# An SSD layer on one core: the chunk scan woven one filling step later, the gate norm behind a whole z tile, three products moved to VectorE

## The chip, the cores and the metric

The kernel runs on one core of one Trainium2 chip. The metric is the device time of one execution in microseconds, lower is better. The engines of the core are named as in the profile: PE is TensorE (matrix products and transposes), DVE is VectorE, ACT is ScalarE, POOL is GpSimd, and SP is the engine that here only issues DMAs. Each engine works through its own instructions in order; engines wait for one another by semaphores.

## The reference, cut to what matters

One inference step of a streaming encoder: a Mamba-2 SSD layer, an MLP, a stick-breaking attention layer and another MLP, each behind an RMS norm and with a residual. There are 1024 prompt tokens and 32 further tokens with cached state, 1056 in all, and the model width is 1024. Only the SSD layer is touched by the change. Its mixer:

```python
zxbcdt = u @ in_w
z, xbc, dt_raw = jnp.split(zxbcdt, [D_INNER, D_INNER + CONV_DIM], axis=-1)
xbc, new_conv = causal_conv(xbc, conv_state, conv_w, conv_b)
...
h_new = h * jnp.exp(a_cs[:, -1])[..., None, None] + jnp.einsum(
    'bsgn,bsgr,bsgrp->bgrpn', b_c, decay_end, xdt_c)
return h_new, y_diag + y_off
```

The input projection gives z, x, B, C and dt. x, B and C go through a causal convolution of four taps and a silu. Then, for each of 8 groups of 4 heads, a recurrence over the tokens is worked out in chunks: inside a chunk by matrix products of C, B and x with decay factors (`y_diag`), from chunk to chunk by a state h (`y_off`). The result, plus D times x, is multiplied by silu(z), RMS-normalised over each group of 256 channels, scaled by `norm_w` and projected back to the model width by `out_w`.

## The kernel before

Activations lie feature-major: 128 features on the partitions, 1056 tokens along the free dimension. Every large product is an fp32 product made of three matmuls of high and low parts. One tile of 128 output features is worked in three column groups of 352 tokens; eight blocks of 128 input features times three matmuls make 24 matmuls per column group. A tile is given out as six **steps** of 12 matmuls. For the tiles of the input projection (`ps_i`) the evacuation out of PSUM is on VectorE: L451 for z, L411 to L415 for x, B and C. Weights are loaded by L137 (`ws_i`) and split in high and low by ACT (L143) and POOL or DVE (L144).

The SSD layer's main loop (from L613) runs over the 8 groups. In round g it builds two lists and weaves them together:

- `main`, the **filling** of TensorE: the two z tiles of group g-1, and the conv tiles B, C, x0 and x1 of group g+1. Between them stand the three parts of the gate norm. Part a (L552 to L554) multiplies the scan's result by z and forms the squares; it belongs to group g-1. Parts b and c belong to group g-2 by then. Part b (L556 to L562) sums the squares over the channels with eight small matmuls (L227, `ss_g`), takes the reciprocal root in eleven small VectorE operations (L560, L214 to L223) and spreads the rows over the partitions by two DMAs, to DRAM and back (L244 `sd_g`, L247 `gs`). Part c (L564 to L568) multiplies by that (two L566 on VectorE, which wait for the second DMA) and stores the two rows `yn_d`. In round 7 the filling is the z tiles of groups 6 and 7, the gate parts, the loads of the residual X0 and X1 (into the places of `s_6x`, the two x tiles of group 6) and the first six steps of the output projection (`ps_o`, evacuated by L658 into X).
- `side`, the **scan** of group g: 9 chunks (the last one the 32 further tokens), each in a stage A and a stage B, in the order A0, A1, B0, A2, B1, ... A8, B7, B8. Stage A of a chunk loads the decay sums `ab` (L470), multiplies B with C and transposes x0, x1 and B into one PSUM tile `pa` (L475 to L478), forms the decay matrix L (POOL L480 adds the mask, ACT L483 takes exp, DVE L484 multiplies), scales x (two L488, `xd`), copies B (ACT L491, `bt`) and scales C by exp(ab) (ACT L493, POOL L494). Stage B forms the state's increment (L509), the part inside the chunk (L514) and the part from the state (L517, which needs h of the chunk before and the product of L494) in a PSUM tile `pb`; POOL L523 forms `ht`, the decayed old state, DVE L525 adds the increment to give h (L520 for chunk 0), and two L528 add the result to x in place.

`weave(main, side, lead)` calls the main steps one by one and, after each, as many scan stages as keep the two lists in proportion; the first `lead` steps pass without any. So `lead` sets how far stage A of chunk 0 stands behind the start of the round.

Stage A of chunk 0 needs the x1 tile of its own group, whose last filling steps end the round before. After them x1 goes through two taps on VectorE (L427 twice, L430, L431), a tanh on ACT (L432, into `cv`) and the closing product on VectorE (L433, into `s_3x` for group 3).

The order on each engine is that in which a scheduler places the instructions of this program; the queues then work in that order. PSUM tiles `pa` and `pb` have two buffers each, `ps_i` and `ps_o` share four; the gate's `gs` tiles have one each.

Of the kernel before, what the change touches and what calls it, by code (L numbers as in the profile page):

```python
# [12 lines left out]
ALU = mybir.AluOpType  # L13
# [52 lines left out]
def weave(main, side, lead=0):  # L66

    n, m = len(main), len(side)
    j = 0
    for i, f in enumerate(main):  # L70
        f()
        want = max(i + 1 - lead, 0) * m // (n - lead)
        while j < want:
            side[j]()
            j += 1
    while j < m:
        side[j]()
        j += 1
# [16 lines left out]
def hybrid_step(ctx: ExitStack, tc: tile.TileContext, xt, cst, cbf, w_in, w_dt, w_out, w_up0, w_dn0, w_qkv, w_o,  # L95
                w_up1, w_dn1, ssm0, ck, cv, y_o, pssm_o, sssm_o, conv_o, pk_o, v_o):
    nc = tc.nc
    ve, sc, gp, te = nc.vector, nc.scalar, nc.gpsimd, nc.tensor
# [199 lines left out]
    def ssd_layer():  # L298
# [4 lines left out]
        with st:  # L303
# [156 lines left out]
            def scan_thunks(g):  # L460
# [4 lines left out]
                def stage_a(c):  # L465
                    w = 128 if c < 8 else 32
                    tk = slice(128 * c, 128 * c + w)
                    B, C, x0, x1 = (slots[g, k] for k in ("B", "C", "x0", "x1"))
                    ab = qp.tile([128, 4, 128], F32, name=f"ab_{g}_{c}", tag="ab", bufs=3)
# [21 lines left out]
                    sc.activation(bt[0:w, :], A[0:w, 384:512], AF.Copy)  # L491
                    if c > 0:
                        sc.activation(ab[:, :, :w], ab[:, :, :w], AF.Exp)  # L493
                        gp.tensor_tensor(ab[:, :, :w], ab[:, :, :w],  # L494
                                         C[:, None, tk].to_broadcast([128, 4, w]), op=ALU.mult)
                    box[c] = (L, xd, bt, ab)

                def stage_b(c):
                    w = 128 if c < 8 else 32
                    tk = slice(128 * c, 128 * c + w)  # L500
                    L, xd, bt, ce = box.pop(c)
                    if c == 8:
                        h = box["h0"]
                    elif c == 0:
                        h = None
                    else:
                        h = box["h"]
# [11 lines left out]
                    if h is None:  # L519
                        ve.tensor_copy(hn, Bp[:, 256:512])  # L520
                    else:
                        ht = qp.tile([128, 256], F32, name=f"ht_{g}_{c}", tag="ht", bufs=1)
                        gp.tensor_tensor(ht.rearrange("p (h d) -> p h d", d=64), h.rearrange("p (h d) -> p h d", d=64),  # L523
                                         een[:, 4 * g:4 * g + 4, c, None].to_broadcast([128, 4, 64]), op=ALU.mult)
                        ve.tensor_tensor(hn, ht, Bp[:, 256:512], op=ALU.add)  # L525
                    for j in range(2):
# [61 lines left out]
            for i, n in enumerate(("ss", "dt", "tails")):  # L588
# [6 lines left out]
                w = min(512, T - 512 * i)  # L595
# [17 lines left out]
            for g in range(8):  # L613
                main, side = [], scan_thunks(g)
                if g > 0:

                    for j in range(2):
                        z = z_tile(g - 1, j)
                        main += z[:2] + gates[:1] + z[2:]
                        gates = gates[1:]  # L620
                    gates = gate(g - 1)
                if g < 7:
                    for k in ("B", "C", "x0", "x1"):
                        if k == "B" and gates:
                            main.append(gates.pop(0))
                        main += conv_tile(g + 1, k)
                else:
                    gt = gates
                    main += gt[0:1] + z_tile(7, 0) + gt[1:2] + z_tile(7, 1, False) + gt[2:3]
                    out0 = late(lambda: down_block(w_out[0], load_o(yn_d, 0, None, stage(0), 1), X, pg, "o0",  # L630
                                                   gmajor=True), 24)
                    main += [lambda: X.extend(load_x(xt, (2, 3, 4, 5, 0, 1, 6, 7), range(2)))] + out0[:6]
                weave(main, side, 2 if g == 7 else 3)
            eng[0] = ve
            dma(conv_o, cvo)
            gt = gate(7)
# [1118 lines left out]
```

## Time and profile before

| | us |
|---|---|
| runs of the kernel | 3014.51, 3011.33, 3012.99 |
| median | 3012.99 |
| the profiled execution, its own time | 3010.28 |
| the span of its profile | 3008.4 |

The granted TensorE clock was 0.992 in the mean. The part that the change touches, the SSD layer's main loop, runs from about 70 to 790 us of the span. There the profile gives for every group from 2 on the same picture, 91.87 us apart (one and the same step of groups 3 and 4 starts at 336.10 and 427.97), so one group stands for the others.

Read the profile in this order: the page for the share of each engine; the list of what TensorE waited for (its rows read "waiting engine, tile and line <- engine, tile and line that released it"); then the timelines of the engines around such a wait (start, duration, engine, line, operation, "[idle time before <- releaser]"; x8 at the end joins eight instructions); and the chain that ended last for the end of group 7.

### The profile page before, as it was taken

The numbers are of one execution on the slowest core, as the hardware profiler recorded it, in microseconds if no ns is written. First come the engines' busy times: TensorE is split into PE (matmuls) and PEld (weight loads), VectorE is DVE, ScalarE is ACT, GpSimd is POOL, SyncE is SP. The second block draws the span as 40 slices with busy tenths as digits, with TensorE's granted clock in tenths as the row PEclk, the third lists the DMA queues.
The fourth block names the chain that finished last, engine by engine and source line by source line (L and its number), as shares of the span: only waits on it lengthen the run. The fifth ranks groups of instructions, "written<-read, shape, count | busy, mean of one in ns | idle before, by whom it ended". The sixth has DMA issues, their size and how long they took to land.

```text
span 3008.4 us, 54983 instructions
## 1 busy us (share of the span) xinstructions
PE 2939.5 (98%) x22262; PEld 2795.8 (93%) x22262; DVE 2270.4 (75%) x3327; ACT 1288.4 (43%) x2207; POOL 626.3 (21%) x525
## 2 busy tenths in 40 slices
PE   9999999999999999999999999999999999999999
PEld 7898999998999999999998888888889999999999
DVE  7877787777748877788776677667677977788776
ACT  4433343434214333444333466666664433344331
POOL 2766656665100000000000123332230000000000
PEclk9999999999999999999999999999999999999999
DMA  4323333324532543365432322222234434464442
GB/s 139 73 54 86 82 85 67 85 79 121 198 93 86 194 140 136 132 205 167 138 97 101 105 73 73 69 68 72 79 100 162 151 137 157 136 206 153 140 131 75
DMA packets 185589, 349.28 MB, mean 116 GB/s; under 512 B 21132, under 2 KB 78328, under 8 KB 185336
## 3 DMA queue, kind: packets, MB, share of 16 engines
q1 hardware_dynamic: 185336, 345.77, 37.4%
q8 instruction: 175, 2.87, 0.4%
q14 instruction: 78, 0.64, 0.1%
HBM read 240.80 MB, written 96.52 MB: 112 GB/s over the span
## 4 chain that ended last, share of the span: by engine, by line
PE 82%; DVE 11%; issue 2%; DMA 2%; ACT 2%; POOL 0%; SPq 0%; DVEq 0%; ACTq 0%; POOLq 0%
PE ps_i L185 15%; PE ps_ua L887 9%; PE ps_ub L887 9%; PE ps_o L185 3%; PE ps_q L185 3%; PE ps_k L185 2%; PE o L1433 2%; PE wt L1417 2%; PE ps_o L166 2%; PE ps_v L185 2%; PE ps_lb L166 2%; PE ps_la L166 2%; PE ps_p L185 1%; DVE p L1380 1%; PE pb L514 1%
## 5 line engine op out<-in xcount | busy, mean ns | idle before, releaser
L185 PE MATMUL ps_i<-xh_n,wh_i 128*128 128x352 f32 x1056 | 356.2, 337 | 0.0
L185 PE MATMUL ps_i<-xh_n,wl_i 128*128 128x352 f32 x1056 | 340.5, 322 | 0.0
L185 PE MATMUL ps_i<-xl_n,wh_i 128*128 128x352 f32 x1056 | 340.2, 322 | 0.0
L1380 DVE TENSOR_TENSOR_SCAN p<-p 128x255 f32<-128x255 f32 (+7 forms) x128 | 193.3, 1511 | 90.8 <-ACT p L1378 89.8
L1382 POOL TENSOR_TENSOR b<-b,p 128x255 f32<-128x255 f32 (+7 forms) x128 | 165.2, 1291 | 379.9 <-DVE p L1380 231.4
L185 PEld LDWEIGHTS ps_i<-xh_n,wh_i 128*128 128x128 f32 x1056 | 198.9, 188 | 13.3 <-issue 12.0
L185 PEld LDWEIGHTS ps_i<-xl_n,wh_i 128*128 128x128 f32 x1056 | 200.2, 190 | 0.0
L185 PEld LDWEIGHTS ps_i<-xh_n,wl_i 128*128 128x128 f32 x1056 | 198.7, 188 | 0.0
L1254 POOL MEMSET qs<- 128x64 f32 x8 | 1.2, 150 | 872.5 <-PE ss_a L227 855.0
L483 ACT ACTIVATE L<-L,naT 128x128 f32<-128x128 f32 (+1 forms) x288 | 90.2, 382 | 154.2 <-POOL L L480 154.1
L1378 ACT ACTIVATE p<-z,qn_q 128x384 f32<-128x384 f32 (+4 forms) x192 | 104.8, 580 | 60.3 <-PE z L1409 29.4
L144 POOL TENSOR_TENSOR wl_i<-ws_i,wh_i 128x1024 fp32r<-128x1024 f32 x44 | 106.8, 2428 | 73.5 <-ACT wh_i L143 73.2
L480 POOL TENSOR_TENSOR L<-ab,cs 128x512 f32<-128x512 f32 (+1 forms) x72 | 106.2, 1475 | 55.0 <-PE pb L514 41.4
L1417 PE MATMUL wt<-cs,b 128*128 128x128 f32 x576 | 90.4, 280 | 15.4 <-DVE wts L1422 12.9
L1378 ACT ACTIVATE b<-z,qn_q 128x384 f32<-128x384 f32 (+4 forms) x192 | 104.4, 585 | 0.0
L738 ACT ACTIVATE d_a<-y_a 128x528 fp32r<-128x528 f32 x105 | 66.8, 640 | 85.5 <-DMA y_a<-q_da 14.0
L738 ACT ACTIVATE d_b<-y_b 128x528 fp32r<-128x528 f32 x105 | 66.4, 639 | 81.6 <-DMA y_b<-q_db 10.9
L1417 PEld LDWEIGHTS wt<-cs,b 128*128 128x128 f32 x576 | 64.9, 140 | 31.2 <-DVE wts L1422 14.5
L739 DVE TENSOR_TENSOR d_a<-y_a,d_a 128x528 fp32r<-128x528 f32 x105 | 73.4, 704 | 19.2 <-ACT d_a L738 19.1
L739 DVE TENSOR_TENSOR d_b<-y_b,d_b 128x528 fp32r<-128x528 f32 x105 | 73.4, 704 | 18.2 <-ACT d_b L738 18.1
L887 PE MATMUL ps_ua<-b_a,wh_a_raw 128*128 128x264 f32 x480 | 77.2, 282 | 0.0
L887 PE MATMUL ps_ub<-b_b,wh_b_raw 128*128 128x264 f32 x480 | 77.2, 282 | 0.0
(1667 smaller groups left out, 9411.1 us busy)
## 6 DMA issues: line engine op xcount, KB each, us to landing
y_a<-q_da SPq DMA_DIRECT2D x98, 264.0 KB, 3.5
y_b<-q_db SPq DMA_DIRECT2D x98, 264.0 KB, 3.4
ws_i<-in_w_in SPq DMA_DIRECT2D x48, 512.0 KB, 3.7
ab<-acs_d SPq DMA_DIRECT2D x64, 256.0 KB, 5.1
ws_a<-in_w_up SPq DMA_DIRECT2D x30, 512.0 KB, 3.7
ws_b<-in_w_up SPq DMA_DIRECT2D x30, 512.0 KB, 3.7
q_da<-t_a SPq DMA_DIRECT2D x26, 528.0 KB, 3.8
q_db<-t_b SPq DMA_DIRECT2D x26, 528.0 KB, 3.4
```

The costliest lines, as they stand in the source:

```text
L144: eng[0].tensor_tensor(lo, st, hi.bitcast(F32), op=ALU.subtract)
L166: te.matmul(box["ps"][g][:, :GW], a[:, c:c + 128], b[:, GRP[g]], start=(k == ks[0] and i == 0), stop=(k == ks[-1] and i == 2))
L185: te.matmul(box["ps"][:, :n], a[:, c:c + 128], b[:, grp[g]], start=(k == 0 and i == 0), stop=(k == nk - 1 and i == 2))
L480: gp.tensor_tensor(L[0:w, :, :w], ab[0:w, :, :w], cs[0:w, None, C_MASK:C_MASK + w].to_broadcast([w, 4, w]), op=ALU.add)
L483: sc.activation(L[0:w, h, :w], L[0:w, h, :w], AF.Exp, bias=naT[0:w, c, 4 * g + h:4 * g + h + 1])
L738: sc.activation(hi, x, AF.Copy)
L739: ve.tensor_tensor(lo, x, hi.bitcast(F32), op=ALU.subtract)
L887: te.matmul(ps[:, g, :QW], a[:, c:c + 128], b[:, QW * g:QW * g + QW], start=(first and n == 0 and i == 0), stop=(n == len(ks) - 1 and i == 2),
L1378: sc.activation(t[0:np_, c:c + w], ps[0:np_, :w], AF.Sigmoid, scale=sn[0:np_, f])
L1380: ve.tensor_tensor_scan(p[0:np_, 1:W][:, ::-1], p[0:np_, 1:W][:, ::-1], p[0:np_, 1:W][:, ::-1], 1.0, op0=ALU.mult, op1=ALU.bypass)
L1382: gp.tensor_tensor(b[0:np_, 0:W - 1], b[0:np_, 0:W - 1], p[0:np_, 1:W], op=ALU.mult)
L1417: te.transpose(ps[:, c, :], self.b[:, 128 * (c0 + c):128 * (c0 + c) + 128], ident)
```

## The change

Four edits, all inside the SSD layer.

```diff
--- before.py
+++ after.py
@@ -491,8 +491,8 @@
                     sc.activation(bt[0:w, :], A[0:w, 384:512], AF.Copy)
                     if c > 0:
                         sc.activation(ab[:, :, :w], ab[:, :, :w], AF.Exp)
-                        gp.tensor_tensor(ab[:, :, :w], ab[:, :, :w],
-                                         C[:, None, tk].to_broadcast([128, 4, w]), op=ALU.mult)
+                        (ve if (g, c) == (7, 8) else gp).tensor_tensor(
+                            ab[:, :, :w], ab[:, :, :w], C[:, None, tk].to_broadcast([128, 4, w]), op=ALU.mult)
                     box[c] = (L, xd, bt, ab)
 
                 def stage_b(c):
@@ -520,7 +520,7 @@
                         ve.tensor_copy(hn, Bp[:, 256:512])
                     else:
                         ht = qp.tile([128, 256], F32, name=f"ht_{g}_{c}", tag="ht", bufs=1)
-                        gp.tensor_tensor(ht.rearrange("p (h d) -> p h d", d=64), h.rearrange("p (h d) -> p h d", d=64),
+                        (ve if g == 7 and c > 6 else gp).tensor_tensor(ht.rearrange("p (h d) -> p h d", d=64), h.rearrange("p (h d) -> p h d", d=64),
                                          een[:, 4 * g:4 * g + 4, c, None].to_broadcast([128, 4, 64]), op=ALU.mult)
                         ve.tensor_tensor(hn, ht, Bp[:, 256:512], op=ALU.add)
                     for j in range(2):
@@ -616,7 +616,7 @@
 
                     for j in range(2):
                         z = z_tile(g - 1, j)
-                        main += z[:2] + gates[:1] + z[2:]
+                        main += z + gates[:1]
                         gates = gates[1:]
                     gates = gate(g - 1)
                 if g < 7:
@@ -630,7 +630,7 @@
                     out0 = late(lambda: down_block(w_out[0], load_o(yn_d, 0, None, stage(0), 1), X, pg, "o0",
                                                    gmajor=True), 24)
                     main += [lambda: X.extend(load_x(xt, (2, 3, 4, 5, 0, 1, 6, 7), range(2)))] + out0[:6]
-                weave(main, side, 2 if g == 7 else 3)
+                weave(main, side, 4)
             eng[0] = ve
             dma(conv_o, cvo)
             gt = gate(7)
```

In words. (1) The weave's lead is 4 steps in every round, instead of 3 (2 in round 7). (2) In each round with z tiles, gate parts b and c stand behind the six steps of their z tile instead of after the first two. (3) In group 7 the small product of L494 for the last chunk, exp(ab) times C (128 x 4 x 32), is given to VectorE. (4) So are, in group 7, the products `ht` of L523 for chunks 7 and 8 (128 x 256).

How the order moves, first on VectorE at the start of round 3. Here `s_3x_3292` is x1 of group 3, `z_3345` the first z tile of group 2, `gs_1` the gate tile of group 1, `L_0` and `xd_0` stage A of chunk 0. Before:

```order
L431 SCALAR_TENSOR_TENSOR s_3x_3292<-pre_90,cwh,cv_3x_3288 128x32
L560 TENSOR_SCALAR gs_1_2677<-ss_g_3347 128x264
L214 TENSOR_SCALAR gs_1_2677<-gs_1_2677 128x264
L215 TENSOR_SCALAR gs_1_2677<-gs_1_2677 128x264
L216 SCALAR_TENSOR_TENSOR gs_1_2677<-gs_1_2677 128x264
L433 SCALAR_TENSOR_TENSOR s_3x_3292<-cv_3x_3288,s_3x_3292 128x1056
L217 TENSOR_TENSOR gs_1_2677<-gs_1_2677 128x264
L451 SCALAR_TENSOR_TENSOR z_3345<-ps_i_1_3366,rstd 128x352
L218 SCALAR_TENSOR_TENSOR gs_1_2677<-gs_1_2677 128x264
L484 TENSOR_TENSOR L_0_3399<-L_0_3399,pa_0_3394 128x512
```
After, the same place:

```order
L431 SCALAR_TENSOR_TENSOR s_3x_3292<-pre_90,cwh,cv_3x_3288 128x32
L433 SCALAR_TENSOR_TENSOR s_3x_3292<-cv_3x_3288,s_3x_3292 128x1056
L451 SCALAR_TENSOR_TENSOR z_3345<-ps_i_1_3347,rstd 128x352
L451 SCALAR_TENSOR_TENSOR z_3345<-ps_i_2_3373,rstd 128x352
L484 TENSOR_TENSOR L_0_3409<-L_0_3409,pa_0_3404 128x512
L488 TENSOR_TENSOR xd_0_3416<-pa_0_3404,dtT 128x256
L488 TENSOR_TENSOR xd_0_3416<-pa_0_3404,ddT 128x256
L455 SCALAR_TENSOR_TENSOR z_3345<-zt_3399,z_3345 128x1056
L560 TENSOR_SCALAR gs_1_2677<-ss_g_3421 128x264
L484 TENSOR_TENSOR L_1_3466<-L_1_3466,pa_1_3461 128x512
L214 TENSOR_SCALAR gs_1_2677<-gs_1_2677 128x264
```
The product L433 that ends x1 now stands directly behind L431. The gate's chain (L560, L214 and on) begins behind the z tile's product L455 and runs through stage A of chunk 1.

Second, on VectorE some twenty rows on, at the two L566 of group 1's gate. `h_1` is the state after chunk 1, `z_3492` the second z tile. Before:

```order
L566 SCALAR_TENSOR_TENSOR s_1x_1281<-s_1x_1281,cs,gs_1_2678 128x1056
L566 SCALAR_TENSOR_TENSOR s_1x_1469<-s_1x_1469,cs,gs_1_2678 128x1056
L484 TENSOR_TENSOR L_2_3528<-L_2_3528,pa_2_3523 128x512
L488 TENSOR_TENSOR xd_2_3535<-pa_2_3523,dtT 128x256
L488 TENSOR_TENSOR xd_2_3535<-pa_2_3523,ddT 128x256
L451 SCALAR_TENSOR_TENSOR z_3492<-ps_i_1_3508,rstd 128x352
L525 TENSOR_TENSOR h_1_3578<-ht_1_3579,pb_1_3568 128x256
L528 SCALAR_TENSOR_TENSOR s_3x_3141<-s_3x_3141,cs,pb_1_3568 128x128
L528 SCALAR_TENSOR_TENSOR s_3x_3292<-s_3x_3292,cs,pb_1_3568 128x128
L451 SCALAR_TENSOR_TENSOR z_3492<-ps_i_2_3555,rstd 128x352
```
After:

```order
L451 SCALAR_TENSOR_TENSOR z_3492<-ps_i_1_3494,rstd 128x352
L484 TENSOR_TENSOR L_2_3550<-L_2_3550,pa_2_3545 128x512
L488 TENSOR_TENSOR xd_2_3557<-pa_2_3545,dtT 128x256
L488 TENSOR_TENSOR xd_2_3557<-pa_2_3545,ddT 128x256
L451 SCALAR_TENSOR_TENSOR z_3492<-ps_i_2_3530,rstd 128x352
L566 SCALAR_TENSOR_TENSOR s_1x_1260<-s_1x_1260,cs,gs_1_2678 128x1056
L566 SCALAR_TENSOR_TENSOR s_1x_1469<-s_1x_1469,cs,gs_1_2678 128x1056
L455 SCALAR_TENSOR_TENSOR z_3492<-zt_3577,z_3492 128x1056
L525 TENSOR_TENSOR h_1_3594<-ht_1_3595,pb_1_3584 128x256
L528 SCALAR_TENSOR_TENSOR s_3x_3141<-s_3x_3141,cs,pb_1_3584 128x128
L528 SCALAR_TENSOR_TENSOR s_3x_3292<-s_3x_3292,cs,pb_1_3584 128x128
```
The two L566 have moved behind the last evacuation L451 of the second z tile; L455 stands right behind them, and L525 of `h_1`, which stood ahead of that evacuation and of L455, now stands behind all of these.

Third, on VectorE at the end of group 7, where `s_6x` are the tiles of gate 6, `wl_o_2` the low part of a weight of the output projection, `xl_y` the low parts of its input, `h_7` and `h_8` the states after chunks 7 and 8. Before:

```order
L566 SCALAR_TENSOR_TENSOR s_6x_5910<-s_6x_5910,cs,gs_6_7314 128x1056
L566 SCALAR_TENSOR_TENSOR s_6x_6061<-s_6x_6061,cs,gs_6_7314 128x1056
L525 TENSOR_TENSOR h_6_7683<-ht_6_7684,pb_6_7673 128x256
L528 SCALAR_TENSOR_TENSOR s_7x_6833<-s_7x_6833,cs,pb_6_7673 128x128
L528 SCALAR_TENSOR_TENSOR s_7x_6984<-s_7x_6984,cs,pb_6_7673 128x128
L484 TENSOR_TENSOR L_8_7754<-L_8_7754,pa_8_7749 32x4x32
L488 TENSOR_TENSOR xd_8_7761<-pa_8_7749,dtT 32x256
L488 TENSOR_TENSOR xd_8_7761<-pa_8_7749,ddT 32x256
L144 TENSOR_TENSOR wl_o_2_7990<-ws_o_2_7987,wh_o_2_7989 128x1024
L205 TENSOR_TENSOR xl_y_8084<-yl_sp_8081,xh_y_8083 128x1056
L205 TENSOR_TENSOR xl_y_8090<-yl_sp_8087,xh_y_8089 128x1056
L525 TENSOR_TENSOR h_7_7806<-ht_7_7807,pb_7_7796 128x256
```
After:

```order
L144 TENSOR_TENSOR wl_o_2_7990<-ws_o_2_7987,wh_o_2_7989 128x1024
L566 SCALAR_TENSOR_TENSOR s_6x_5910<-s_6x_5910,cs,gs_6_7293 128x1056
L566 SCALAR_TENSOR_TENSOR s_6x_6061<-s_6x_6061,cs,gs_6_7293 128x1056
L525 TENSOR_TENSOR h_6_7727<-ht_6_7728,pb_6_7717 128x256
L528 SCALAR_TENSOR_TENSOR s_7x_6833<-s_7x_6833,cs,pb_6_7717 128x128
L528 SCALAR_TENSOR_TENSOR s_7x_6984<-s_7x_6984,cs,pb_6_7717 128x128
L484 TENSOR_TENSOR L_8_7768<-L_8_7768,pa_8_7763 32x4x32
L488 TENSOR_TENSOR xd_8_7775<-pa_8_7763,dtT 32x256
L488 TENSOR_TENSOR xd_8_7775<-pa_8_7763,ddT 32x256
L494 TENSOR_TENSOR ab_8_7761<-ab_8_7761,s_7C 128x4x32
L523 TENSOR_TENSOR ht_7_7821<-h_6_7727,een 128x256
L205 TENSOR_TENSOR xl_y_8084<-yl_sp_8081,xh_y_8083 128x1056
```
The weight's L144 has moved ahead of the two L566, and L494 and the first L523 stand between them and `h_7`, which follows one L205 later; the second L523 and a third L205 come after that, ahead of `h_8`.

On TensorE the gate's L227 (`ss_g`) stands behind stage A of chunk 0, where it stood behind the first 24 matmuls of the z tile. On SP's queue the weight load L137 that stood between the spread's two DMAs (L244 and L247) in rounds 2 to 6 now stands ahead of both.

## The prediction

> **What bounds the kernel now.** The page comes first, for the share of each engine.
>
> ```profile
> span 3008.4 us, 54983 instructions
> PE 2939.5 (98%) x22262; PEld 2795.8 (93%) x22262; DVE 2270.4 (75%) x3327; ACT 1288.4 (43%) x2207; POOL 626.3 (21%) x525
> ```
>
> TensorE (PE) is busy for 98% of the span, and the change adds and removes no matmul. It can move the time only through the microseconds in which TensorE waits. The second view is the list of what PE waited for in the first 1200 us, which hold the whole SSD stage (columns: us in total, times, longest).
>
> ```profile
> PE pa L477 <- DVE s_2x L433: 2.9, 1, 2.9
> PE pb L517 <- POOL ab L494: 2.2, 1, 2.2
> PE ps_o L185 <- DVE X_in_xt L658: 1.9, 1, 1.9
> PE pa L477 <- DVE s_3x L433: 1.8, 1, 1.8
> PE pa L477 <- DVE s_4x L433: 1.8, 1, 1.8
> PE pa L477 <- DVE s_5x L433: 1.8, 1, 1.8
> PE pa L477 <- DVE s_7x L433: 1.8, 1, 1.8
> PE pa L477 <- DVE s_6x L433: 1.8, 1, 1.8
> PE pa L477 <- DVE s_0x L433: 1.5, 1, 1.5
> PE pa L477 <- DVE s_1x L433: 1.5, 1, 1.5
> ```
>
> In each of the eight groups the transpose of x1 in stage A of chunk 0 (L477) waits until VectorE has finished x1's silu (L433): 2.9 + 5 x 1.8 + 2 x 1.5 = 14.9 us. The rows with L494 and L658 are the end of group 7. The sum thus has three kinds of term: these waits, waits that the new order makes, and the end of group 7.
>
> **Lead and gate part: the waits that go (L633, L619).** The third view is the timeline of group 3, VectorE, ScalarE and TensorE around that wait.
>
> ```profile
> 333.00 1.08 ACT L432 ACTIVATE cv_3x<-s_3x 128x1056 f32<-128x1056 f32 x1 [5.24 <-DVE s_3x L431]
> 334.36 1.25 DVE L433 SCALAR_TENSOR_TENSOR s_3x<-cv_3x,s_3x 128x1056 f32<-128x1056 f32 x1
> 335.67 0.33 PE L477 MATMUL pa<-cs,s_3x 128*128 128x128 f32 x1 [1.84 <-DVE s_3x L433]
> 335.83 0.27 PE L478 MATMUL pa<-cs,s_3B 128*128 128x128 f32 x1
> 339.78 0.38 PE L475 MATMUL pa<-s_3C,s_3B 128*128 128x128 f32 x2
> ```
>
> Without the wait L477 would have run at 335.67 - 1.84 = 333.83. From L478 to the next stage A lie 24 matmuls of the filling, 339.78 - 335.83 = 3.95 us, so one step of 12 is 1.96 us. Now six steps stand ahead of stage A of chunk 0 instead of four, while the column sum L227 (about 0.6 us) goes behind it: it comes to L477 at 333.83 + 3.92 - 0.6 = 337.2. L433 can start when the tanh ends, 334.08, and the four gate instructions that stood ahead of it are gone: it ends at 335.4. That leaves 1.8 us to spare in groups 3 to 6, about 0.4 in group 2 (3.3 more against 2.9), and 1.96 - 1.5 = 0.4 in groups 0 and 1, where one step is added. In group 7 three steps are added. I take all eight waits as gone: **-14.9 us**. If a group's margin is not there, it keeps part of its 1.5 to 2.9.
>
> Group 2 has something behind its wait.
>
> ```profile
> 242.32 0.48 PE L477 MATMUL pa<-cs,s_2x 128*128 128x128 f32 x1 [2.87 <-DVE s_2x L433]
> 242.59 0.42 PE L478 MATMUL pa<-cs,s_2B 128*128 128x128 f32 x1
> 247.90 0.39 PE L475 MATMUL pa<-s_2C,s_2B 128*128 128x128 f32 x2
> 200.00:250.00 50.00, 47.13 (x325) 43.73 (x325) 40.77 (x64) 18.44 (x34) 26.32 (x24) 0.97 0.27 64
> ```
>
> The same 24 matmuls took 247.90 - 242.59 = 5.31 us instead of 3.95, with a granted clock (the column 0.97) below 1 in that stretch: the wait of 2.87 us cost **1.4 us** more, which goes with it. The Trainium skill ("TensorE: Matmul & The Clock Gate", section "What's actually happening") gives half clock after an idle window of about 3.4 us; by it a wait of 2.87 us need cost nothing and the sum would be 1.4 us smaller, but the rows of this trace show the dip after the shorter wait, and the measurement decides; that result, 3003.9, lies within the case that I forecast.
>
> In group 0 the copy of B for chunk 1 (L491) now stands behind the tanh L432 on ScalarE. The 1.08 us of L432 bounds it; most of it lies beside the filling, and I take 0.3.
>
> **The same edits: the wait they can make.** The gate part that moves issues eight small matmuls, eleven VectorE operations (L560, L214 to L223), two DMAs of the spread (L244, L247), and behind it come two L566 and two stores (L568). All of it begins later. On VectorE the two L566, which wait for the spread, and the z product L455 now stand ahead of the state h of chunk 1 (L525), which stage B of chunk 2 needs (L517); before, h came behind L566 too, but with time to spare.
>
> ```profile
> 336.64 0.68 DVE L484 TENSOR_TENSOR L<-L,pa 128x512 f32<-128x512 f32 x1
> 339.38 0.43 DVE L223 SCALAR_TENSOR_TENSOR gs<-gs 128x264 f32<-128x264 f32 x1
> 343.41 0.33 SPq L137 DMA_DIRECT2D ws_i<-in_w_in  x1
> 343.83 0.38 SPq L247 DMA_DIRECT2D gs<-sd_g  x1
> 344.57 2.44 POOL L552 TENSOR_TENSOR s_2x<-s_2x,z 128x1056 f32<-128x1056 f32 x1 [1.19 <-DVE z L455]
> 348.26 2.93 DVE L566 SCALAR_TENSOR_TENSOR s_1x<-s_1x,cs,gs 128x1056 f32<-128x1056 f32 x2 [1.92 <-DMA gs<-sd_g]
> 360.53 0.39 PE L517 MATMUL pb<-ab,h 128*64 128x128 f32 x4
> 796.50 0.43 DVE L223 SCALAR_TENSOR_TENSOR gs<-gs 128x264 f32<-128x264 f32 x1
> 802.25 1.32 DVE L566 SCALAR_TENSOR_TENSOR s_7x<-s_7x,cs,gs 128x1056 f32<-128x1056 f32 x1
> L455 DVE SCALAR_TENSOR_TENSOR z<-zt,z x16: 1243/2600/2892, 155.6 to 760.7; 128x1056 f32<-128x1056 f32 x16
> ```
>
> L517 of that stage comes one step later and without the wait: 360.53 + 1.96 - 1.84 = 360.65. VectorE's side, walked from the last z evacuation at 336.6: that evacuation and stage A of chunk 0 (0.5, then L484's 0.68 and two products like L525's 0.41), L455 at 2.6 (its median; 1.24 when GpSimd is idle) to 341.2, then 2.4 of GpSimd's product L552, beside which the first gate operation may stand still as L494 does below, to 343.7, then thirteen short operations (L223's 0.43 at most, less where they overlap) to some 348.9. The spread took 348.26 - 339.81 = 8.45 us before, because its second DMA stood on SP's queue behind L137, which waited; where nothing stood ahead it took 802.25 - 796.93 = 5.3. In the new order L137 stands ahead of both, where its wait is over by then, so I take 5.3: L566 from 354.2 to 357.1, L455 to 358.4 or 359.7, h at 358.8 or 360.1. The need is at 360.65, so the margin is 0.5 to 1.8 us, within the error of such a walk: bounds 0 and, with a spread of 8.45, 360.1 + 3.15 - 360.65 = 2.6 us in each of six groups. I take 0.4 each, **+2.5 us**.
>
> **Two products on VectorE, and the end of group 7 (L494, L523).** Rows of GpSimd, TensorE, VectorE, and of the chain that ended last.
>
> ```profile
> 761.91 2.54 DVE L566 SCALAR_TENSOR_TENSOR s_6x<-s_6x,cs,gs 128x1056 f32<-128x1056 f32 x2
> 764.37 0.41 DVE L525 TENSOR_TENSOR h<-ht,pb 128x256 f32<-128x256 f32 x1
> 764.47 4.02 DMA yn_d<-s_6x
> 766.25 4.47 POOL L494 TENSOR_TENSOR ab<-ab,s_7C 128x128 f32<-128x128 f32 x1 [1.50 <-ACT ab L493]
> 766.87 1.20 DVE L144 TENSOR_TENSOR wl_o<-ws_o,wh_o 128x1024 fp32r<-128x1024 f32 x1
> 768.00 2.41 DVE L205 TENSOR_TENSOR xl_y<-yl_sp,xh_y 128x1056 fp32r<-128x1056 f32 x2
> 768.56 4.51 DMA X_in_xt<-in_xt
> 770.78 0.31 PE L517 MATMUL pb<-ab,h 128*64 128x32 f32 x4 [2.22 <-POOL ab L494]
> 773.55 15.78 PE ps_o L185 x84
> ```
>
> GpSimd's small L494 took 4.47 us because L144 and L205 ran on VectorE meanwhile; on VectorE it should take about 0.35 (near the L525 row's 0.41 for twice the width), and the two L523 0.41 each: 1.2 us more on VectorE, and the wait of 2.22 goes. But TensorE then waits for the same end as before: L185 needs a PSUM slot, which L658 frees once X0 is loaded into the place of s_6x, and that follows L566, the store of 4.02 and the load of 4.51. So removing 2.22 us gains nothing by itself. And L566 comes later: a product L144 (1.20) now stands ahead of it, and h of chunk 3 with its two L528 (1.0, of which 0.3 found a gap) is now done behind the gate's column sum, on a VectorE without a gap. That is 1.9 us, so L658 goes from 773.1 to 775.0. VectorE itself, with 1.2 + one further L205 (1.2) ahead of L658, is there at 775.3. TensorE resumes near 775.6 instead of 773.55: 2 us. Its 84 matmuls took 15.78 instead of 84 x 1.96 / 12 = 13.7 after two waits of 2.2 and 1.9; a longer one can cost up to 2 more, half of it taken: **+3 us**, bounds 0 (L144 falls into a gap) and 6 (the load collides with the weights' load).
>
> **Sum.** -14.9 - 1.4 + 0.3 + 2.5 + 3 = -10.5 us. Against the profiled execution's own 3010.28 us this is 2999.8. The median of the runs, 3012.99, lies 2.71 above that execution, so for a median I say **3002.5 us**.
>
> **Rivals.**
> - All waits go and none comes: -16.3 + 0 to 1.5 in group 7, 2996.7 to 2998.2. For it: every margin in the walk is positive. Against: the X0 chain is bound to L566.
> - The new wait for h is 1 to 2.5 us in groups 2 to 7, 6 x 1.75 = 10.5 instead of 2.5: -2.5, 3010.5. For it: the margin of 0.5 us in the slow case, and L455's median of 2.6.
> - Slower: the same place, with the spread at 8.45 us or more because SP's queue is held up there too. It decides when L223 to L566 exceeds 5.8 us in the slow case of L455. Then 6 x 2.6 = 15.6, and a wait of that size has the 1.4 us of group 2 behind it: 6 x 1.4 = 8.4. With 0.3 + 5 in group 7 that is -16.3 + 29.3 = +13, 3026. Against: L137 has left the place between the spread's DMAs.
> - The change does not do what it says: stage A of chunk 0 still waits in groups 0 to 2, where 0.4 us is to spare, and the end of group 7 keeps its wait under the name L658. About half of 5.9 + 1.4 comes back, -7, 3006.
>
> **Chances.** Forecast 0.43 (2998 to 3006), all gone 0.18, waits for h 0.20, slower 0.08, partly 0.11. The measurement of this kernel can tell some 0.2%, 6 us, from no change: under 3007 is faster, over 3019 slower. Faster: 0.43 + 0.18 + 0.05 of the partial case = 0.66; slower 0.07; the rest 0.27. The range 2994 to 3012 leaves out the slower case and the edges.
>
> **What would show it.** In the list of waits: no row L477 from L433 (part 1); a row L517 from DVE h L525 in groups 2 to 7 if the spread is late, with L566 directly behind "DMA gs" on VectorE; the row L517 from POOL L494 gone, and L658's grown from 1.9 to 4 or more. The windows at 200 to 250 should show clock 1.00. The forecast is wrong if L223 to L566 takes over 6 us, or if x1's silu still comes last in a group with 0.4 us to spare.

## The result, and the profile after

The changed kernel took 2995.81 us (median of 6 runs, 2993.78 to 3000.29) against 3012.01 (median of 6 runs of before, 3004.58 to 3014.51): a ratio of 0.995, 95% interval 0.9939 to 0.996, 16 us less. In a later comparison the same kernel took 2998.78 against 3011.3, ratio 0.9958 (0.9944 to 0.9972), 13 us less. The forecast was 3002.5, 10.5 less.

First the page of the kernel after.

```profile
span 2991.5 us, 54964 instructions
PE 2932.9 (98%) x22262; PEld 2789.3 (93%) x22262; DVE 2278.7 (76%) x3330; ACT 1286.2 (43%) x2207; POOL 637.1 (21%) x522
```

The matmuls are as many as before, the span is 16.9 us shorter. Next the list of what TensorE waited for in the first 1200 us, after (columns as before: in all, times, longest).

```profile
PE ps_o L185 <- DVE X_in_xt L658: 4.1, 1, 4.1
PE pb L517 <- DVE h L525: 2.1, 6, 0.5
PE pb L509 <- DVE s_7x L528: 1.1, 1, 1.1
PE ps_o L185 <- DVE xl_y L205: 0.9, 1, 0.9
PE pb L509 <- ACT bt L491: 0.5, 1, 0.5
PE pa L477 <- DVE s_0x L433: 0.5, 1, 0.5
```

Seven of the eight rows L477 are gone, and group 0 keeps 0.5. The new row is L517 from h, 2.1 us in six small pieces; L494 is gone, and L658 has grown from 1.9 to 4.1. Before, these rows and their like came to 14.9 + 2.2 + 1.9 = 19.0 us; now they come to 9.2, which is 9.8 less. (A second execution of each kernel, below, gives 19.6 and 10.4, 9.2 less.)

Where does that stand in the span? A good landmark is the first of the matmuls of the first MLP shown here (L887 with `b_a`; the MLP itself begins 8.7 us ahead of it, in both kernels): up to there lies all that the change touches, behind it instructions that the change leaves alone. Before, then after (the numbers ahead of the semicolon are its first and last start):

```profile
L887 PE MATMUL ps_ua<-b_a,wh_a_raw x480: 278/283/285, 986.6 to 1282.4; 128*128 128x264 f32 x160
```

```profile
L887 PE MATMUL ps_ua<-b_a,wh_a_raw x480: 278/283/285, 976.6 to 1272.4; 128*128 128x264 f32 x160
```

The SSD stage thus gave 10.0 us in this pair of executions, and 16.9 - 10.0 = 6.9 us came from later stages whose instructions are the same. So there were two questions for the experiments: which edit brings the 10 us, and where the other 6.9 come from. Two stretches of the same work in the attention stage show the latter's face (last columns: granted TensorE clock, DMA share, GB/s). Before:

```profile
1650.00:1700.00 50.00, 48.33 (x299) 44.49 (x297) 24.01 (x54) 18.01 (x41) 3.46 (x7) 0.93 0.33 91
```

After, the same work, ten us earlier, and the stretch of group 2:

```profile
200.00:250.00 50.00, 50.00 (x356) 46.39 (x354) 41.61 (x61) 18.59 (x38) 31.27 (x25) 1.00 0.31 76
1640.00:1690.00 50.00, 48.33 (x318) 43.85 (x318) 25.95 (x58) 20.75 (x49) 4.32 (x8) 1.00 0.34 97
```

TensorE was as busy in both (48.33 us), but before it had a clock of 0.93: 0.07 x 50 = 3.5 us lost there. In what follows, a stretch in which the granted clock falls below 1 is called a clock dip.

### The profile page after: what moved, and what is told of

It is laid out like the page before. It is cut to its first block, busy times and chain, and to the rows that moved or that the text cites. A ratio compares the mean times of both kernels' runs of the same rounds, so it can differ in the third digit from the quotient of the medians.

```text
span 2991.5 us, 54964 instructions
## 1 busy us (share of the span) xinstructions
PE 2932.9 (98%) x22262; PEld 2789.3 (93%) x22262; DVE 2278.7 (76%) x3330; ACT 1286.2 (43%) x2207; POOL 637.1 (21%) x522
## 3 DMA queue, kind: packets, MB, share of 16 engines
q8 instruction: 175, 2.87, 0.4%
## 4 chain that ended last, share of the span: by engine, by line
PE 66%; DVE 7%; issue 2%; DMA 2%; ACT 2%; POOL 1%; SPq 0%; DVEq 0%; ACTq 0%; POOLq 0%
PE ps_ua L887 9%; PE ps_ub L887 9%; PE ps_q L185 3%; PE ps_o L185 3%; PE ps_i L185 2%; PE ps_k L185 2%; PE o L1433 2%; PE wt L1417 2%; PE ps_o L166 2%; PE ps_lb L166 2%; PE ps_la L166 2%; PE ps_v L185 2%; PE ps_p L185 1%; DVE p L1380 1%; PE ps_k L166 1%
## 5 line engine op out<-in xcount | busy, mean ns | idle before, releaser
L185 PEld LDWEIGHTS ps_i<-xh_n,wh_i 128*128 128x128 f32 x1056 | 198.3, 188 | 13.1 <-issue 12.5
L480 POOL TENSOR_TENSOR L<-ab,cs 128x512 f32<-128x512 f32 (+1 forms) x72 | 115.1, 1599 | 49.7 <-PE pb L514 28.6
L144 POOL TENSOR_TENSOR wl_i<-ws_i,wh_i 128x1024 fp32r<-128x1024 f32 x44 | 106.7, 2426 | 49.6 <-ACT wh_i L143 49.4
L1417 PE MATMUL wt<-cs,b 128*128 128x128 f32 x576 | 90.3, 280 | 14.9 <-DVE wts L1422 12.4
L658 DVE TENSOR_TENSOR X_in_xt<-X_in_xt,ps_o 128x352 f32<-128x352 f32 x72 | 35.6, 518 | 54.9 <-PE ps_o L185 31.6
L887 PE MATMUL ps_ub<-b_b,wh_b_raw 128*128 128x264 f32 x480 | 77.3, 283 | 0.0
```

Source lines behind the costliest of these rows:

```text
L144: eng[0].tensor_tensor(lo, st, hi.bitcast(F32), op=ALU.subtract)
L185: te.matmul(box["ps"][:, :n], a[:, c:c + 128], b[:, grp[g]], start=(k == 0 and i == 0), stop=(k == nk - 1 and i == 2))
L480: gp.tensor_tensor(L[0:w, :, :w], ab[0:w, :, :w], cs[0:w, None, C_MASK:C_MASK + w].to_broadcast([w, 4, w]), op=ALU.add)
L887: te.matmul(ps[:, g, :QW], a[:, c:c + 128], b[:, QW * g:QW * g + QW], start=(first and n == 0 and i == 0), stop=(n == len(ks) - 1 and i == 2),
L1417: te.transpose(ps[:, c, :], self.b[:, 128 * (c0 + c):128 * (c0 + c) + 128], ident)
```

## The experiments

In the table "first L887" is that landmark in the one profiled execution of a run (in p6, p12 and w_pad the same line has the number 893 or 889), and "rest" is the span less it. Each ratio is to runs of before in the same comparison, whose medians were 3011.3 to 3012.0.

| kernel | median us (runs) | ratio to before, 95% | first L887 | rest |
|---|---|---|---|---|
| before | 3012.01 (6) | | 986.6 | 2021.8 |
| changed | 2995.81 (6) | 0.995 (0.9939 to 0.996) | 976.6 | 2014.9 |
| e1_lead | 3004.94 (11) | 0.9976 (0.9964 to 0.9989) | 981.2 | 2015.4 |
| e2_gate | 3008.0 (11) | 0.9992 (0.9983 to 1.0001) | 986.3 | 2020.2 |
| e3_prod | 3009.76 (11) | 0.9999 (0.999 to 1.0008) | 989.2 | 2018.5 |
| e4_noprod | 2999.98 (5) | 0.9968 (0.9956 to 0.9981) | 978.5 | 2019.7 |
| p6 | 3001.58 (7) | 0.9964 (0.9952 to 0.9976) | 979.3 | 2017.9 |
| p12 | 3001.07 (9) | 0.9965 (0.9954 to 0.9976) | 978.4 | 2021.7 |
| c_before (before again) | 3018.28 (1) | | 991.5 | 2024.9 |
| c_after (changed again) | 2998.78 (6) | 0.9958 (0.9944 to 0.9972) | 978.2 | 2018.7 |
| w_pad | 3010.19 (12) | 0.9996 (0.9986 to 1.0006) | 988.4 | 2022.6 |
| e5_x0 | 2992.53 (6) | 0.9934 (0.992 to 0.9949) | 970.8 | 2019.1 |
| e5_again (the same) | 2990.48 (6) | 0.9933 (0.9918 to 0.9948) | 970.4 | 2019.3 |

**The lead alone.**

```diff
-                weave(main, side, 2 if g == 7 else 3)
+                weave(main, side, 4)
```

> The lead alone (4 in every round), all else as before. Order: in round 3 TensorE has 60 filling matmuls and the gate's column sum ahead of stage A of chunk 0 (48 and the sum before). Theory S (only TensorE's waits in the SSD stage count): one step of 1.96 us more covers the 1.5 and 1.8 us waits of L477 on L433, group 2 keeps 2.9 - 2.0 = 0.9; h of chunk 1 stays ahead of L455 and behind an early gate norm, so no wait at L517. The first MLP (first L887) begins 13 to 15 us earlier, less 0 to 2 for the end of group 7. Theory C (the granted clock in the later, unchanged stages decides as much): the time from the first L887 to the end differs from before's by several us, as it did after the change (2021.8 before, 2014.9 after), and not by the same amount in every kernel; theory S says it is the same within 1 us in all kernels and the 7 us were one execution's chance.

The landmark came 5.4 us earlier, not 13 to 15. The timeline of group 3, VectorE before, then GpSimd, VectorE and TensorE in this kernel:

```profile
332.73 0.24 DVE L431 SCALAR_TENSOR_TENSOR s_3x<-pre,cwh,cv_3x 128x32 f32<-128x32 f32 x1
```

```profile
327.38 2.27 POOL L494 TENSOR_TENSOR ab<-ab,s_3C 128x512 f32<-128x512 f32 x1
328.42 1.28 DVE L431 SCALAR_TENSOR_TENSOR s_3x<-pre,cwh,cv_3x 128x32 f32<-128x32 f32 x1
329.62 0.42 DVE L560 TENSOR_SCALAR gs<-ss_g 128x264 f32<-128x264 f32 x1
331.09 1.25 DVE L433 SCALAR_TENSOR_TENSOR s_3x<-cv_3x,s_3x 128x1056 f32<-128x1056 f32 x1
332.40 0.33 PE L477 MATMUL pa<-cs,s_3x 128*128 128x128 f32 x1 [0.97 <-DVE s_3x L433]
```

L560 and its followers still stand ahead of L433, and L431 took 1.28 us (0.24 in the kernel before) beside GpSimd's L494, so 0.97 us of the wait is left in each of six groups, and 0.5 in group 0: 6.3 of the 14.9. At the end of group 7 the list has L658 at 4.9. The step of 1.96 us does not pay in full alone, because the product L433 is held up on VectorE.

**The gate parts alone.**

```diff
-                        main += z[:2] + gates[:1] + z[2:]
+                        main += z + gates[:1]
```

> The gate parts alone (behind all six steps of their z tile), leads and products as before. Order: in round 3 stage A of chunk 0 comes after 60 matmuls and no column sum, and L433 stands directly behind L431. Theory S: in groups 2 to 7 stage A comes 1.96 - 0.6 = 1.4 us later and L433 ends 1.3 us earlier, so those six waits (11.9 us, and 1.4 of clock in group 2) go but for some 0.2 in group 2; groups 0 and 1 keep 1.5 each, having no gate part. L517 waits for h of chunk 1 0 to 0.3 in each. First L887 11 to 13 us earlier, the end of group 7 giving back 0 to 2. Theory C as for the lead alone.

The landmark stayed (986.3), against an expected 11 to 13 us: the clearest miss. From this kernel's list of waits, and VectorE in its group 3:

```profile
PE pb L517 <- DVE h L525: 6.0, 6, 1.3
PE ps_o L185 <- DVE X_in_xt L658: 3.5, 1, 3.5
PE pa L477 <- DVE s_7x L433: 2.1, 1, 2.1
PE pa L477 <- DVE s_3x L433: 0.5, 1, 0.5
```

```profile
349.73 0.43 DVE L223 SCALAR_TENSOR_TENSOR gs<-gs 128x264 f32<-128x264 f32 x1
355.43 2.28 DVE L566 SCALAR_TENSOR_TENSOR s_1x<-s_1x,cs,gs 128x1056 f32<-128x1056 f32 x1 [3.56 <-DMA gs<-sd_g]
```

The waits at L477 fell to 0.5 in groups 3 to 6 only. Group 7 has 2.1 (its lead is still 2), groups 0 to 2 have 1.5 to 1.7, where for group 2 some 0.2 was expected: in all 8.8 of the 14.9. And L517 now waits for h, 1.0 in a group: VectorE stands still for 3.56 us at L566 until the spread is in, and h stands behind L566. Behind the gate's column sum the scan comes to L517 a step sooner here than with the longer lead. So in TensorE's waits the two edits need each other: the gate part frees L433, the lead moves the scan away from the late gate. Of the 14.9 us the lead alone leaves 6.3, the gate alone 8.8 + 6.0 = 14.8, both (below) 0.5 + 2.3 = 2.8.

The times do not show this. By the landmark the gains are 5.4 and 0.3 us apart and 8.1 together, but against a second execution of before (991.5, below) they are 10.3, 5.2 and 13.0; by the ratios of the medians they are 7.2, 2.4 and 9.6, each uncertain by 3 to 4 us. That the two give more together than apart is shown for the waits, and not for the time.

**The products alone, and the change without them.**

```diff
-                        gp.tensor_tensor(ab[:, :, :w], ab[:, :, :w],
+                        (ve if (g, c) == (7, 8) else gp).tensor_tensor(ab[:, :, :w], ab[:, :, :w],
...
-                        gp.tensor_tensor(ht.rearrange("p (h d) -> p h d", d=64), h.rearrange(...
+                        (ve if g == 7 and c > 6 else gp).tensor_tensor(ht.rearrange("p (h d) -> p h d", d=64), h.rearrange(...
```

> The three products on VectorE alone (L494 of the last chunk, L523 for chunks 7 and 8 of group 7), weave and gate as before. Theory S: the wait of 2.2 us at L517 for L494 goes, and L185's wait for L658 grows from 1.9 to 3.5 to 5, because the load of X0 sets the end: first L887 0 to 1 us later, no gain. Rival: GpSimd's 4.5 us in L494 was the hole, and L658 does not grow: first L887 2 us earlier. Theory C: from the first L887 to the end, a number other than 2021.8 by several us.

The rows are those of theory S: the wait at L517 is gone, and L658 stands at 3.6.

```profile
PE ps_o L185 <- DVE X_in_xt L658: 3.6, 1, 3.6
```

But this is no effect of the edit. The kernel before, run a second time (c_before, below), has no row L494 either, and the same L658:

```profile
770.45 0.46 POOL L494 TENSOR_TENSOR ab<-ab,s_7C 128x128 f32<-128x128 f32 x1 [1.49 <-ACT ab L493]
PE ps_o L185 <- DVE X_in_xt L658: 3.6, 1, 3.6
```

Of the six profiled executions that have this product on GpSimd, only the first shows it at 4.47 us; the other five have 0.46 to 1.19 and no wait for it. The hole that edit (3) was to close was a chance of one execution. Nor does e3_prod show that the load of X0 sets the end: VectorE has no gap in the 6 us until L658 begins (L523 from 775.78 for 0.41, L658 at 776.11), so it may have come last itself.

The landmark is 2.6 us later than in the first profile, but this execution also began its group 0 some 1.7 us later (its first L477 runs at 85.1 instead of 83.4), which lies ahead of anything that differs; c_before began it at 85.4. The time is that of before (ratio 0.9999).

The edits of the lead and the gate without these two lines (e4_noprod):

> Lead and gate parts changed, the three products left on GpSimd: the change without its first two edits. Theory S: the eight waits of L477 are gone and L517 waits for h of chunk 1 some 0.35 in six groups, as after the change; in the end of group 7 a wait at L517 for L494 of about 2 returns and L658's falls from 4.1 to about 2, so the first L887 comes where it does after the change (976.6) within 1 us. Rival: the products were worth 2 us or more, and it comes at 978.6 or later. Theory C: from the first L887 to the end a number between 2014 and 2022 that goes with the granted clock, not with the change.

The landmark is at 978.5, 1.9 us behind one execution of the changed kernel (976.6) and 0.3 behind the other (978.2). It misses theory S's range by 0.9 and the rival's by 0.1. The wait for L494 did not come back, as it was no rule before: L658 stands there with 4.9, behind two products L552 on VectorE (761.93 for 2.42). So the products are worth between 0 and 2 us, not told apart from nothing; the 10 us come from lead and gate together.

**What the later stages do by themselves.** Two kernels add only time: 6 or 12 products of zeros on TensorE behind group 7 (the diff shows 6).

```diff
+            def pad():
+                ps = pa.tile([128, 512], F32, name="pad", tag="pb", bufs=2)
+                for _ in range(6):
+                    te.matmul(ps, zero[:, :128], zero, start=True, stop=True)
...
-            run(main[:5] + gt[1:2] + main[5:10] + gt[2:] + main[10:])
+            run(main[:5] + gt[1:2] + main[5:10] + gt[2:] + main[10:20] + [pad] + main[20:])
```

> The changed kernel with 6 products of zeros (128x512 bf16, into a PSUM tile that nobody reads) put into the output projection after group 7, where TensorE is dense: at full clock some 0.2 us each, so everything behind begins 1.3 us later and nothing else moves. Theory C1 (each execution draws its clock dips by chance): median 1.3 us above the changed kernel's 2995.8, within 1.5, and the time from the first L887 to the end as often 2015 as 2020. Theory C2 (where the dips fall is fixed by when the later stages begin): the median lies elsewhere by up to 7 us, and its runs stay as close together as the changed kernel's. If neither holds and the 6 us belong to the change's own waits, 2997.1 too.

> As p6 with 12 such products: everything behind begins 2.6 us later. C1: median 2998.4 within 1.5. C2: a median that is off this by several us, in either direction, and another granted clock in the stretches of the attention stage (1640 to 1690) than in the changed kernel.

Both medians, 3001.58 and 3001.07, lie over what C1 allowed from the changed kernel's 2995.8, and they do not go up with the padding. That looked like C2, but the sign that it named, another clock in the attention stage, is missing: from 1650 to 1700 both have 1.00, like the changed kernel in its first profile. The two kernels were then run again without any change.

> The kernel before once more, unchanged, for a second profiled execution. C1: the granted clock around 1650 to 1700, 0.93 in the first profile, is as likely 1.00, and the time from the first L887 to the end lies between 2014 and 2022 by chance. C2: it is 0.93 again and that time 2021.8 within 1.

> The changed kernel once more, unchanged. Theory C1 (waits in the SSD stage are fixed, the clock dips of the attention stage fall by chance): first L887 at 976.6 within 1; from there to the end anywhere from 2014 to 2022, since ten profiled executions of nine kernels gave 2014.9 to 2024.9 with a mean of 2019.4; median of many runs 976.6 + 2019.4 + 2.2 (execution less span) = 2998.2 within 2, above the first six runs' 2995.8. Theory C2 (the dips of the later stages are fixed by the kernel): 2014.9 again within 1, median 2995.8 within 1.

The kernel before had its first L887 at 991.5 this time, 4.9 us later than in the first profile, with the same instructions. Its one run, 3018.28, is longer than all 19 other runs of before in that comparison (up to 3017.69). Its clock in four stretches, then its wait in group 0, which was 1.5 in the first profile:

```profile
50.00:100.00 50.00, 46.35 (x291) 44.11 (x290) 44.42 (x62) 18.45 (x37) 24.05 (x23) 0.97 0.29 69
200.00:250.00 50.00, 47.13 (x331) 43.56 (x328) 40.53 (x66) 18.40 (x38) 27.27 (x25) 0.97 0.29 68
300.00:350.00 50.00, 48.16 (x330) 44.43 (x328) 41.82 (x63) 17.18 (x34) 24.83 (x22) 0.97 0.27 64
1650.00:1700.00 50.00, 48.33 (x287) 45.57 (x286) 22.84 (x53) 14.86 (x29) 1.61 (x4) 0.90 0.32 91
```

```profile
PE pa L477 <- DVE s_0x L433: 2.4, 1, 2.4
```

Three of its eight waits for L433 (groups 0, 2 and 3) have a clock dip behind them, where the first profile had one (group 2). Of the 4.9 us, 2.0 are there at the first L477 (85.43 against 83.39), 0.9 of them the longer wait of group 0. The dips behind groups 0 and 3 bring 1.6 each, as the same rows of groups 1 and 4 show, and the end of group 7 gives 0.7 back. Its rest, 2024.9, lies outside both forecasts, C2's 2021.8 within 1 and C1's 2014 to 2022.

The changed kernel, run again, had a rest of 2018.7 instead of 2014.9, and a median of 2998.78, where C1 said 2998.2 within 2 and C2 2995.8 within 1. Its landmark, 978.2, misses C1's 976.6 within 1: the wait at L658 was 5.2 instead of 4.1, so the waits are not fixed either. From 1650 to 1700 two executions of one and the same kernel had clocks of 0.93 and 0.90 (before), 1.00 and 0.97 (changed), 0.93 and 1.00 (e5). So C2 falls, and of C1 the part stands that dips come by chance, over a wider range than it said: the first profile of the changed kernel was a lucky one, with the lowest rest of thirteen executions (2014.9 to 2024.9, mean 2019.6).

**How long a wait must be for the clock to dip.** From the thirteen profiles I took each wait of TensorE in the SSD stage that stands alone, and the granted clock in the 8 us behind it; a dip reads 0.79 or 0.80 there behind a wait at L477 (0.21 x 8 = 1.7 us lost) and 0.63 to 0.79 behind L658.

| wait | seen | with a dip |
|---|---|---|
| 0.9 to 1.7 us | 29 | 0 |
| 1.8 to 1.9 us | 16 | 2 |
| 2.0 to 2.5 us | 3 | 1 |
| 2.87 us (group 2) | 3 | 3 |
| 3.4 to 5.2 us (L658) | 10 | 10 |

In the last two rows the length goes with the place: every wait of 2.87 us is that of group 2, every longer one the end of group 7. The table alone doesn't tell the length from what else is special there.

The Trainium skill ("TensorE: Matmul & The Clock Gate", section "What's actually happening") gives half clock after an idle window of about 3.4 us and says that the window runs freely, so that the same kernel shows different numbers of slow matmuls at its start. The last row agrees; the rows of 1.8 to 2.87 us show dips after waits that are shorter than such a window.

To try this by itself, the kernel before got products of zeros where it waits:

```diff
+                    for _ in range(8 if c == 0 else 0):
+                        te.matmul(A, zero[:, :128], zero, start=True, stop=True)
                     te.matmul(A[0:w, 0:w], B[:, tk], C[:, tk], start=True, stop=True)
```

> The kernel before with 8 products of zeros (128x512 bf16, into the PSUM tile pa that the next matmul overwrites) ahead of stage A of chunk 0 in every group: TensorE works for about 1.7 us where it waited for L433. The waits in the page shrink to 0 to 0.3 (group 2: 1.2), the time they took does not come back. Theory W (idle TensorE, not only late work, costs: a wait of 1.8 us drops the granted clock now and then, one of 2.4 to 2.9 mostly): clock 1.00 behind every stage A of chunk 0, first L887 at 985 to 987, where the kernel before had 986.6 and 991.5 with one and three dips; median 2 to 4 us under the kernel before, all of it the clock. Theory N (only the waits count): first L887 between 986 and 992 as before, median the same within 1 or up to 1.5 later, since in groups 0 and 1 the padding is longer than the wait.

Its waits of that kind:

```profile
PE pa L479 <- DVE s_7x L433: 1.9, 1, 1.9
PE pa L479 <- DVE s_2x L433: 1.1, 1, 1.1
PE pa L479 <- DVE s_0x L433: 0.7, 1, 0.7
```

No dip stands behind stage A of chunk 0 in any group, that of group 2 included, which had one in each of the three executions with its full wait. But the landmark (988.4) and the median (1.1 us under before, ratio 0.9986 to 1.0006) show no gain that can be measured: W's 985 to 987 and its 2 to 4 us did not come, and N's landmark of 986 to 992 did. In group 0 the wait with its padding is as long as in c_before, in group 7 the wait of 1.9 stays behind the padding, because the scheduler placed the filling otherwise. The run supports theory W's clock for group 2, in one execution, and its gain in time is not shown.

**A version that is faster than both.** By its chain, the end of group 7 in the changed kernel hangs on the load of X0 into the place of `s_6x`. The places of B and C of group 6 are free much earlier, if the z tiles of group 7 do not take them:

```diff
-                        return hx.tile([128, T], F32, name=f"z_{g}{j}", tag=f"h{j}")
+                        return qp.tile([128, T], F32, name=f"z_{g}{j}", tag=f"x2{j}", bufs=1)
...
-(2, 3, 4, 5, 0, 1, 6, 7)
+(0, 1, 4, 5, 2, 3, 6, 7)
```

(The second pair stands at the three places that name the order of X.)

> The changed kernel with X0 and X1 loaded into the places of B and C of group 6 (free since that group's scan), and the z tiles of group 7 in the places of x0 and x1 of group 5 instead. Order: SP issues the loads of X0 and X1 some thirty rows earlier, ahead of the gate's spread. Theory S (the end of group 7 hangs on X0, behind L566 and its store): L658's wait of 4.1 us goes, and the clock dip behind it (84 matmuls 15.3 us instead of 13.7): what is left is a wait of 0.5 to 2 at L517 for h of chunk 8. First L887 at 976.6 - 4 = 972.6 within 1.5. Rival: VectorE, not the load, is last there (h of chunk 8 was ready at 763.4, L658 at 763.43), and the gain is under 1 us. Whole time: 2 to 6 us under the changed kernel, less or more by what the later clock does.

> The version with X0 and X1 in the places of B and C of group 6, beside the changed kernel on one chip. First L887 at 970.8 within 1, median 4 to 7 us under the changed kernel's in this comparison: 4.1 of the wait for X0 and some 1.6 of the clock behind it.

The row L658 is gone from its list of waits, and behind the end of the scan TensorE is busy at full clock:

```profile
755.00:765.00 10.00, 10.00 (x79) 8.79 (x78) 10.00 (x22) 1.32 (x2) 0.00 (x0) 1.00 0.93 332
765.00:775.00 10.00, 10.00 (x68) 9.35 (x66) 10.00 (x15) 2.18 (x2) 0.00 (x0) 1.00 0.22 74
```

The landmark is at 970.8 and 970.4, 5.8 to 7.8 us ahead of the changed kernel's two, a little more than theory S's 972.6 within 1.5 allowed, and on one chip the medians are 2990.48 and 2998.78: 8.3 us less, somewhat over the 4 to 7 expected. The rival's gain of under 1 us is out, but not its cause. VectorE's L658 in the changed kernel, in its second execution, and here:

```profile
763.43 1.38 DVE L658 TENSOR_TENSOR X_in_xt<-X_in_xt,ps_o 128x352 f32<-128x352 f32 x3
764.97 1.81 DVE L658 TENSOR_TENSOR X_in_xt<-X_in_xt,ps_o 128x352 f32<-128x352 f32 x4 [1.10 <-DMA X_in_xt<-in_xt]
752.43 0.51 DVE L658 TENSOR_TENSOR X_in_xt<-X_in_xt,ps_o 128x352 f32<-128x352 f32 x1
```

In the changed kernel the load landed last, but VectorE came to L658 only 0 to 1.1 us sooner. By these rows a load that landed in time would alone have given no more than that. With the new places the first L658 also stands elsewhere in VectorE's order, ahead of L566, and the gain is that of both.

## Why the prediction was right, and where its size was off

- **The eight waits of L477 (-14.9).** They went, but for 0.5 in group 0. In group 3 of the changed kernel L433 ends before TensorE comes:

```profile
321.31 5.43 DVE L427 SCALAR_TENSOR_TENSOR cv_3x<-pre,cwh,cv_3x 128x1059 f32<-128x1059 f32 x2 [0.67 <-ACT cv_3x L425]
330.29 1.26 DVE L433 SCALAR_TENSOR_TENSOR s_3x<-cv_3x,s_3x 128x1056 f32<-128x1056 f32 x1 [1.15 <-ACT cv_3x L432]
331.72 0.27 PE L477 MATMUL pa<-cs,s_3x 128*128 128x128 f32 x1
```

  L433 now waits for the tanh alone, as predicted. But the spare time was 0.2 us, not 1.8: from 330.29 + 1.26 to 331.72. The taps L427 of x1 were begun 1.2 us later than the walk has them, 0.67 of it in waiting for ScalarE's L425, and took 5.43. Before, they followed without a wait and took 5.03:

```profile
325.54 5.03 DVE L427 SCALAR_TENSOR_TENSOR cv_3x<-pre,cwh,cv_3x 128x1059 f32<-128x1059 f32 x2
```

  The margin was mis-sized, and that 0.2 was enough was luck. Group 0 kept 0.5 because its wait is 2.4 in c_before and e3_prod, and one step takes 1.96 of it; the 1.5 of the first profile was that execution's.

- **The copy in group 0 (+0.3).** 0.5 at L509 for L491.

- **The wait for h (+2.5).** 2.1, in six groups. The walk is confirmed in its order, in the same group:

```profile
344.21 0.42 DVE L223 SCALAR_TENSOR_TENSOR gs<-gs 128x264 f32<-128x264 f32 x1
349.72 4.70 DVE L566 SCALAR_TENSOR_TENSOR s_1x<-s_1x,cs,gs 128x1056 f32<-128x1056 f32 x2 [2.35 <-DMA gs<-sd_g]
354.33 1.25 DVE L455 SCALAR_TENSOR_TENSOR z<-zt,z 128x1056 f32<-128x1056 f32 x1
355.50 0.41 DVE L525 TENSOR_TENSOR h<-ht,pb 128x256 f32<-128x256 f32 x1
356.06 0.44 PE L517 MATMUL pb<-ab,h 128*64 128x128 f32 x4 [0.46 <-DVE h L525]
```

  From L223's end to L566 lie 349.72 - 344.63 = 5.1 us, where 5.3 was taken and 8.45 was the bad case: with L137 ahead of both, SP's queue was free. The two L566 took 4.7 instead of 2.9, and L455 behind them 1.25 instead of up to 2.6. So two rows were off by over a microsecond in opposite directions, and that the term came out so near is in part luck.

- **The end of group 7 (+3).** From the gate's column sum to TensorE's return it was 773.55 - 738.90 = 34.65 us before. The column sum before, and the rows of the changed kernel:

```profile
738.90 0.66 PE L227 MATMUL ss_g<-gs,ones 128*32 128x264 f32 x8
```

```profile
726.80 0.65 PE L227 MATMUL ss_g<-gs,ones 128*32 128x264 f32 x8
733.43 0.42 DVE L560 TENSOR_SCALAR gs<-ss_g 128x264 f32<-128x264 f32 x1
753.59 2.53 DVE L566 SCALAR_TENSOR_TENSOR s_6x<-s_6x,cs,gs 128x1056 f32<-128x1056 f32 x2
754.92 3.76 DMA yn_d<-s_6x
758.70 4.71 DMA X_in_xt<-in_xt
764.01 15.33 PE ps_o L185 x84
```

  764.01 - 726.80 = 37.2 us, 2.6 more, where 2 was forecast. The 1 us more for a longer dip did not come: the 84 matmuls took 15.33 instead of 15.78. The chain ends as predicted (L566, store, load, L658), with VectorE free only just before the load landed. L560 came 6.6 us behind the column sum, against 0.8 before; this need not have cost anything, since VectorE came to L566 without a gap. The two further waits in group 7 (L509 for L528, 1.1; L205, 0.9) were not foreseen. With them TensorE's waits at the end of group 7 went from 4.1 to 6.1 us, in the second pair from 3.6 to 7.1.

  The prediction read L494's 4.47 us as what GpSimd pays beside L144 and L205, and its wait of 2.2 as a part of the kernel. It was not there in the second execution of before. As the prediction gave its removal no gain, the sum does not suffer from it.

- **The sum for the stage** was -10.5 by the profiled execution, and the landmark moved by 10.0. The median of 2995.8 lies nearer to the rival in which all waits go and none comes (2996.7 to 2998.2). The list of waits decides against that rival: 2.1 us at L517 came, and 2.2 more at L658.

- **What was mis-sized is what one execution cannot tell, the clock above all.** The prediction gave the clock 1.4 us, the dip of group 2, and held everything else at that execution's. But other waits that went could bring a dip too: the second execution of before had two more (3.2 us) and 0.9 more of waiting in group 0, and its landmark 991.5 lies 13.3 us behind the changed kernel's second (978.2). The mean of the two executions of each is 989.05 and 977.4, so the change gave some 11.7 us in the stage, with one to three dips in it; the second execution of before, longer than the other runs of that kernel, makes this rather too large. The prediction also took the difference of one pair of executions for that of the medians, while the time behind the landmark varies by ten us with the same instructions.

What stays open: 16.2 and 12.5 us between medians against 11.7 in the stage leave 1 to 5 us. (The three kernels beside the changed one that have both lead and gate, e4_noprod, p6 and p12, have medians 10 to 12 us under 3012, the padding included, so 16.2 stands at the high end.) Two profiled executions of each kernel, with rests of 2021.8 and 2024.9 before and 2014.9 and 2018.7 after, do not tell whether the change also makes dips in the later stages rarer; kernels in between have 2015.4 to 2022.6.

## What to carry to other kernels

When an engine is 98% busy, the list of its waits is the whole budget, and an edit that moves one producer earlier has to be read together with what is queued behind it: here the gate alone only moved the waits, from 14.9 to 14.8 us, the lead alone left 6.3, and both left 2.8. Where two things come in close together at the end of a chain (here a load and VectorE's own queue), removing one gains little; follow the chain to the tile whose place is needed, free that place, and see what moves with it. And take more than one profiled execution of both kernels, before a few us in untouched stages are given a cause and before an edit is made for a wait: the 2.2 us for L494 stood in one of two executions of the same kernel.

## What the runs showed of the hardware

A TensorE wait of 1.8 or 1.9 us cost up to 1.7 us more behind it, by a clock dip that came in 2 of 16 cases, in all 3 at 2.87 us (one place, group 2) and in none of 29 up to 1.7 us. So in these runs the price of a wait was its own length up to 1.7 us, and about one and a half times that at 2.87. Two such dips were 3.2 of the 4.9 us by which two executions of the same kernel differed in the SSD stage.
